# A fused encoder layer on one core: one weight unit's low parts go to VectorE, a low part and its products go ahead of a scaling, and the gates' product goes two units later

## The chip, the cores and the metric

One core of one Trainium2 chip runs the whole kernel. The metric is the device time of one execution in microseconds, as the median of three runs: 691.59 us before the change (691.51 to 693.78). All times below count from the start of the span of the profiled execution, in us, unless they are durations.

The engines are TensorE (PE in the profile), VectorE (DVE), ScalarE (ACT), GpSimd (POOL) and SyncE (SP), which here only issues transfers.

## The reference, cut to what matters

The layer normalises x, projects it by one wide matrix, runs two token mixers and merges them. The change touches the normalisation, the first group of projected columns (sq, the attention's queries) and the gates mi and mf.

```python
h = rmsnorm(x, norm_w)                       # x: 512 tokens of 1024 channels, float32
proj = jnp.einsum('bsd,de->bse', h, w_in) + b_in
(mq, mk, mv, mi, mf, mo, mz, sq, sk, sv, sz, gates) = jnp.split(proj, split_at, axis=-1)
...
log_i = mi.astype(jnp.float32).transpose(0, 2, 1)
log_f = jax.nn.log_sigmoid(mf.astype(jnp.float32)).transpose(0, 2, 1)
...
qs = rmsnorm(to_heads(sq, SB_HEADS), sb_q_norm_w)
ks_ = rmsnorm(to_heads(sk, SB_HEADS), sb_k_norm_w)
os_ = stick_breaking_attention(qs, ks_, to_heads(sv, SB_HEADS))
```

## The kernel before

**Tiles and products.** The 512 tokens are four blocks (tb = 0 to 3) of 128; the 1024 channels are eight slices (k = 0 to 7) of 128. Every float32 operand is split into a high part in a rounded format and a low part, the rest; a product of two operands is three matmuls of 512 columns (high by high and the two mixed ones). The normalised and turned x lies in `hh` (high) and `hl` (low). Weights are fetched in units of 512 KB into `stg` (three buffers); ACT copies the high part (`wh`), DVE subtracts the low part (`wl`), lines 97 and 98.

**The head.** The first group (units 0 to 3, queries of attention heads 0 to 3) is special: each unit holds two slices k, `first_split` (L1141) makes their high parts `fh` on ACT and their low parts `fl` on DVE for units 0 and 2, on POOL for units 1 and 3 (L1147). Unit 3 is fetched into a buffer with the tag P5, so its tile reads `P`. Per block of x, `x_scale` (L277) has ACT make the sum of squares, POOL the reciprocal root (`rstd`, L274 and L275, result in `xs`) and DVE scale x in place (L290). `x_turn` (L292) has PE transpose the block in eight pieces (L300, into two PSUM tiles `aps`), DVE make `hh` (L302, four slices at once) and `hl` (L306, one slice at a time).

**The order.** All is written out by hand: each engine runs its instructions in the order in which the code issues them, and waits there for what it needs. The code issues the work ahead of the loop (L1149 to L1177), then loops over the units c = 0, 1, 2, ...: evacuation of unit c-1's sums, deferred functions due at c, fetches and splits up to unit c+2 (`ahead`), the first half of unit c's products (`mm(0)`), waiting pieces, the attention heads' steps, the second half (`mm(1)`). In the head, unit c's products are block tb = c over all eight k (`first_mm`, L1181): k = 0 to 3 in `mm(0)`, 4 to 7 in `mm(1)`. `x_turn(1)` stands between the halves of c = 0, and behind it `x_scale(2)` and `x_scale(3)`; `x_turn(2)` and `x_turn(3)` stand in c = 1. The sums of the first group get a bias row `brow`, fetched from DRAM, on DVE (L347, `qraw`).

**The gates.** `gates_prep` (due at c = 3) makes the high and low part of the gates' weights (`wg`) on DVE. `gates` (due at c = `GATES_START`, 4) runs 16 matmuls (L573, L574), one copy on ACT (L576), one sum on DVE (L578), and two stores to DRAM issued by SP (`i_d` and `f_d`, L580 and L581). Those are read again at c = 35 (`gates_scan`).

**Behind it on SP.** The queries are turned for the attention in two parts: DVE transposes 32 by 32 blocks (`ty`, L388), one unit later SP issues sixteen small transfers (`tz`, L398), and still later DVE multiplies `tz` by a weight `qkw` (L402). The first part's `tz` are issued at c = 6, the second's at c = 8. Units 4 to 7 are the keys `kraw`; DVE scales them by their norm `rk` (L369, eight instructions for two blocks, twice). At c = 10 the first head starts: PE transposes the four blocks of `kraw` (L438) between the halves of unit 10.

Of the kernel before, what the change touches and what calls it, by code (L numbers as in the profile page):

```python
# [8 lines left out]
F32 = mybir.dt.float32  # L9
FR = mybir.dt.float32r  # L10
BF = mybir.dt.bfloat16
AF = mybir.ActivationFunctionType
OP = mybir.AluOpType
# [3 lines left out]
KT = 8  # L17
# [8 lines left out]

SB_START = [10, 13, 16, 20, 26, 28, 32, 34]
M_START = [52, 56, 70, 76]
GATES_PREP, GATES_START, GATES_SCAN = 3, 4, 35
TURNED = {("q", 0, 0), ("q", 0, 1), ("q", 1, 0), ("q", 1, 1), ("k", 0, 1), ("k", 1, 1)}  # L30
REST = {11, 16, 20, 23, 24, 32, 44, 64}
AHEAD, LOADS = 2, 4
# [3 lines left out]
def tile_hybrid_layer(  # L36
# [16 lines left out]
    nc = tc.nc  # L53
# [21 lines left out]
    def blk(tag, dt=F32, shape=(512,), name=None, p=128):  # L75

        where = mp if tag in MISC else sp
        return where.tile([p] + list(shape), dt, name=name or tag, tag=tag, bufs=BUFS[tag])

    def two(tag, dt=F32, name=None):  # L80

        t = blk(tag, dt, (2, 512), name=name)
        return t[:, 0, :], t[:, 1, :]

    def dense_ps():
        return psd.tile([128, 512], F32, name="dps", tag="dps")

    def att_ps():
        return psa.tile([128, 512], F32, name="aps", tag="aps")
# [40 lines left out]
    units = []  # L130
# [59 lines left out]
    def h_sta(k, tb):  # L190
        ts = slice(tb * 128, (tb + 1) * 128)
        return hh[:, k, ts], hl[:, k, ts]
# [8 lines left out]
    x_t = []  # L201
# [16 lines left out]
    ident = cst.tile([128, 128], F32, name="ident")  # L218
# [8 lines left out]
    nw_t = cst.tile([128, 8], F32, name="nw_t")  # L227
# [42 lines left out]
    hh = hp.tile([128, KT, T], FR, name="hh", tag="hh")  # L270
    hl = hp.tile([128, KT, T], FR, name="hl", tag="hl")

    def rstd(dst, ssq, n, eps):
        nc.gpsimd.tensor_scalar(dst, ssq, 1.0 / n, eps, op0=OP.mult, op1=OP.add)  # L274
        nc.gpsimd.tensor_tensor(dst, dst, mhalf[:, 0:dst.shape[1]], op=OP.pow)  # L275

    def x_scale(tb):  # L277
        xs = tiny.tile([128, 4], F32, name="xs", bufs=2)
        ssq, r = xs[:, 0:2], xs[:, 2:3]
        xn = x_t[tb]  # L280
        junk = blk("om", BF, (D,), name="junk")
        if tb == 0:
            for i in range(2):
                c = slice(i * D // 2, (i + 1) * D // 2)
                nc.scalar.activation(junk[:, c], xn[:, c], AF.Square, accum_out=ssq[:, i:i + 1])
            nc.gpsimd.tensor_tensor(ssq[:, 0:1], ssq[:, 0:1], ssq[:, 1:2], op=OP.add)
        else:
            nc.scalar.activation(junk, xn, AF.Square, accum_out=ssq[:, 0:1])
        rstd(r, ssq[:, 0:1], D, EPS)
        nc.vector.tensor_scalar(xn, xn, r, None, op0=OP.mult)  # L290

    def x_turn(tb):  # L292
        ts = slice(tb * 128, (tb + 1) * 128)
        xn = x_t[tb]
        for g in range(2):
            ks = slice(4 * g, 4 * g + 4)
            tp = att_ps()
            for j in range(4):
                kt = g * 4 + j
                nc.tensor.transpose(tp[:, j * 128:(j + 1) * 128], xn[:, kt * 128:(kt + 1) * 128], ident)  # L300
            dh = hh[:, ks, ts]
            nc.vector.tensor_tensor(dh, tp.rearrange("p (k t) -> p k t", k=4),  # L302
                                    nw_t[:, ks].unsqueeze(2).to_broadcast([128, 4, 128]), op=OP.mult)
            for j in range(4):
                k = 4 * g + j
                nc.vector.scalar_tensor_tensor(hl[:, k, ts], tp[:, j * 128:(j + 1) * 128], nw_t[:, k:k + 1],  # L306
                                               hh[:, k, ts].bitcast(F32), op0=OP.mult, op1=OP.subtract)

    def bias_row(c0):
        b = blk("brow")  # L310
# [242 lines left out]
    def gates_fill():  # L553
        wg = blk("P5", FR, (KT, 128), name="wg")
        nc.gpsimd.memset(wg.bitcast(F32), 0.0)
        wg_t.append(wg)
# [513 lines left out]
    u = []  # L1070
# [67 lines left out]

    f_w = []

    def first_split(i, low=None):  # L1141
        u = units[i]
        his = two("qk", FR, name="fh")
        for j in range(2):
            hi, lo = his[j], blk("y", FR, name="fl")
            nc.scalar.activation(hi, u.st[:, j, :], AF.Copy)
            (low or nc.vector).tensor_tensor(lo, u.st[:, j, :], hi.bitcast(F32), op=OP.subtract)  # L1147
            f_w.append((hi, lo))

    units[0].load()  # L1150
    units[1].load()
# [12 lines left out]
    def warm(n):  # L1164
        for _ in range(n):
            nc.tensor.matmul(wp, idle[:, 0:128], idle, start=True, stop=True)

    warm(9)
    norm_vec()
    x_scale(0)  # L1170
    warm(2)
    first_split(0)
    x_turn(0)
    first_split(1, nc.gpsimd)
    x_scale(1)
    first_split(2)
    first_split(3, nc.gpsimd)  # L1177

    f_ps = []

    def first_mm(tb):  # L1181
        def mm(half):
            if half == 0:
                f_ps.append(dense_ps())
            for k in range(4 * half, 4 * half + 4):
                sh, sl = h_sta(k, tb)
                wh, wl = f_w[k]
                nc.tensor.matmul(f_ps[tb], sh, wh, start=k == 0, stop=False)
                nc.tensor.matmul(f_ps[tb], sl, wh, start=False, stop=False)
                nc.tensor.matmul(f_ps[tb], sh, wl, start=False, stop=k == KT - 1)  # L1190
        return mm
# [36 lines left out]
    def ahead(c):  # L1228
        while count["ready"] < min(N, c + AHEAD + 1):
            fetch(count["ready"] + 1)  # L1230
            units[count["ready"]].split()
            count["ready"] += 1
        fetch(c + LOADS + 1)

    for c in range(N):
        now[0] = c
        if 0 < c < TB:
            ahead(c)
        if c and units[c - 1].slow:
            units[c - 1].slow()  # L1240
            ahead(c)
        due = later.pop(c, [])
        if c > n_proj - 9:
            ahead(c)
        if c:
            units[c - 1].evac()
        for fn in due:
            fn()
        ahead(c)
        units[c].mm(0)  # L1250
        if c < 2:
            x_turn(c + 1)
        if c == 0:
            x_scale(2)
            x_scale(3)
            gates_fill()
        for g in list(act):
            if c in REST:
                continue
            if next(g, "end") == "end":  # L1260
                act.remove(g)
        for e in list(pend):
            if c >= e[0] and e[2]():
                pend.remove(e)
                g = e[3]()
                next(g)
                act.append(g)
        units[c].mm(1)
        if c == 1:
            x_turn(3)  # L1270
# [31 lines left out]
```

## Time and profile before

| | us |
|---|---|
| median of three runs | 691.59 |
| lowest and highest run | 691.51, 693.78 |
| the profiled execution's own time | 692.46 |
| its span | 690.7 |
| PE busy | 682.2 |
| DVE busy | 467.5 |
| ACT busy | 337.1 |
| POOL busy | 115.3 |

The span goes from the first to the last instruction. Busy time of PE counts matmuls that overlap once; a matmul of 512 columns is shown with some 0.39 us, but the next one starts 0.23 us after it. A row of the timeline gives the start, the duration, the engine, the line, the operation and its operands, and in brackets the idle time of the engine ahead of it with what ended it, if that is known; `x8` are eight such instructions in a row.

### The profile page before, as it was taken

How to read it: one execution, taken by the hardware profiler on the slowest of the kernel's cores; microseconds unless marked ns; L12 is line 12 of the kernel's file. 1: busy time of each engine (PE TensorE's matmuls, PEld its weight loads, DVE VectorE, ACT ScalarE, POOL GpSimd, SP SyncE). 2: the span in 40 equal slices, each digit the busy share in tenths (PEclk: the TensorE clock that was granted, in tenths of full speed). 3: DMA queues.
4: the chain of work that ended last, by engine and by line, in shares of the span. 5: the costliest groups of instructions: out<-in, count | busy, mean ns of one | idle time of the engine just before them, and what ended most of it. 6: DMA issues, size and time to landing. Idle time of an engine off the chain costs nothing.

```text
span 690.7 us, 9388 instructions
## 1 busy us (share of the span) xinstructions
PE 682.2 (99%) x3162; PEld 568.9 (82%) x3162; DVE 467.5 (68%) x817; ACT 337.1 (49%) x631; POOL 115.3 (17%) x268
## 2 busy tenths in 40 slices
PE   7999999999999999999999999999999999999997
PEld 4878888888888888888888888888888888888876
DVE  6745687777997886679834748994352364445997
ACT  6235364576554663244466434447554343344451
POOL 5222022365440310000011110000112000111020
PEclk9999999999999999999999999999999999999999
DMA  7423534535553533553332333434323455489333
GB/s 249 138 92 107 155 108 127 148 71 151 158 149 106 135 106 90 112 121 92 106 108 61 91 105 104 117 92 125 88 62 91 113 179 196 135 194 222 121 82 102
DMA packets 122289, 84.74 MB, mean 123 GB/s; under 512 B 19018, under 2 KB 105956, under 8 KB 122240
## 3 DMA queue, kind: packets, MB, share of 16 engines
q1 hardware_dynamic: 119600, 77.97, 40.2%
q0 software_dynamic: 2496, 6.03, 4.5%
q8 instruction: 25, 0.41, 0.2%
q14 instruction: 24, 0.20, 0.1%
q10 hardware_dynamic: 144, 0.13, 0.1%
HBM read 66.22 MB, written 2.15 MB: 99 GB/s over the span
## 4 chain that ended last, share of the span: by engine, by line
PE 94%; DMA 2%; DVE 2%; POOL 1%; SPq 0%; ACT 0%; issue 0%; DVEq 0%; ACTq 0%
PE dps L92 27%; PE dps L93 27%; PE dps L94 27%; PE aps L93 3%; PE aps L94 3%; PE aps L92 3%; DMA P<-in_w_in_dram 1%; DMA brow<-in_b_in_dram 1%; PE aps L794 1%; PE aps L796 1%; PE aps L795 1%; DVE hl L306 1%; POOL fl L1147 0%; DVE hh L302 0%; DVE wl L98 0%; PE aps L573 0%
## 5 line engine op out<-in xcount | busy, mean ns | idle before, releaser
L98 DVE TENSOR_TENSOR wl<-stg,wh 128x1024 fp32r<-128x1024 f32 x92 | 112.6, 1224 | 107.6 <-ACT wh L97 107.4
L92 PE MATMUL dps<-hh,wh 128*128 128x512 f32 x448 | 175.0, 391 | 0.0
L94 PE MATMUL dps<-hh,wl 128*128 128x512 f32 x448 | 174.4, 389 | 0.0
L93 PE MATMUL dps<-hl,wh 128*128 128x512 f32 x448 | 174.4, 389 | 0.0
L97 ACT ACTIVATE wh<-stg 128x1024 fp32r<-128x1024 f32 x92 | 96.8, 1052 | 65.3 <-PE dps L94 45.1
L94 PEld LDWEIGHTS dps<-hh,wl 128*128 128x128 f32 x448 | 84.1, 188 | 17.7
L93 PEld LDWEIGHTS dps<-hl,wh 128*128 128x128 f32 x448 | 84.2, 188 | 16.8
L92 PEld LDWEIGHTS dps<-hh,wh 128*128 128x128 f32 x448 | 84.1, 188 | 16.8
L92 PE MATMUL dps<-wh,hh 128*128 128x512 f32 x224 | 87.7, 392 | 0.0
L94 PE MATMUL dps<-wh,hl 128*128 128x512 f32 x224 | 87.3, 390 | 0.0
L93 PE MATMUL dps<-wl,hh 128*128 128x512 f32 x224 | 87.2, 389 | 0.0
L94 PEld LDWEIGHTS dps<-wh,hl 128*128 128x128 f32 x224 | 42.0, 188 | 9.0
L92 PEld LDWEIGHTS dps<-wh,hh 128*128 128x128 f32 x224 | 42.1, 188 | 8.3
L93 PEld LDWEIGHTS dps<-wl,hh 128*128 128x128 f32 x224 | 42.1, 188 | 8.2
L687 DVE SCALAR_TENSOR_TENSOR acc<-tmp,vec,acc 128x511 f32<-128x511 f32 (+2 forms) x48 | 36.0, 750 | 1.7
L690 ACT ACTIVATE tmp<-acc 128x512 f32<-128x512 f32 x16 | 10.1, 634 | 50.8 <-DVE acc L687 50.8
L463 POOL TENSOR_SCALAR_AFFINE_SELECT om<-om 128x128 f32<-128x128 f32 x32 | 15.3, 479 | 96.2 <-ACT om L461 96.1
L469 DVE TENSOR_TENSOR_SCAN om<-om 128x512 f32<-128x512 f32 (+3 forms) x32 | 26.7, 834 | 5.5 <-POOL om L463 5.5
L747 POOL TENSOR_SCALAR_AFFINE_SELECT w_all<-om 128x128 f32<-128x128 f32 x16 | 5.7, 386 | 143.6 <-DMA om<-rb_d 129.4
L461 ACT ACTIVATE om<-aps,rq 128x512 f32<-128x512 f32 (+3 forms) x32 | 16.8, 524 | 21.0 <-PE aps L94 21.0
L92 PE MATMUL dps<-yh,wh 128*128 128x512 f32 x64 | 24.9, 389 | 0.0
L93 PE MATMUL dps<-yl,wh 128*128 128x512 f32 x64 | 24.9, 389 | 0.0
(249 smaller groups left out, 1222.2 us busy)
## 6 DMA issues: line engine op xcount, KB each, us to landing
stg<-in_w_in_dram SPq DMA_DIRECT2D x87, 512.0 KB, 3.9
az<-ay SPq DMA_DIRECT2D x128, 40.0 KB, 3.2
stg<-in_w_proj_s_dram SPq DMA_DIRECT2D x8, 512.0 KB, 4.3
B<-in_w_out_dram SPq DMA_DIRECT2D x8, 512.0 KB, 5.8
stg<-in_w_proj_m_dram SPq DMA_DIRECT2D x8, 512.0 KB, 5.5
wl<-stg POOLq DMA_DIRECT2D x8, 512.0 KB, 5.8
tz<-ty SPq DMA_DIRECT2D x72, 32.0 KB, 1.9
brow<-in_b_in_dram SPq DMA_DIRECT2D x8, 256.0 KB, 4.4
```

The lines of the kernel that those rows point to most:

```text
L92: nc.tensor.matmul(ps, ah, bh, start=first, stop=False)
L93: nc.tensor.matmul(ps, ah, bl, start=False, stop=False)
L94: nc.tensor.matmul(ps, al, bh, start=False, stop=last)
L97: nc.scalar.activation(hi, src, AF.Copy)
L98: nc.vector.tensor_tensor(lo, src, hi.bitcast(F32), op=OP.subtract)
L306: nc.vector.scalar_tensor_tensor(hl[:, k, ts], tp[:, j * 128:(j + 1) * 128], nw_t[:, k:k + 1], hh[:, k, ts].bitcast(F32), op0=OP.mult, op1 ...
L461: nc.scalar.activation(om[:, 0:n], zp, AF.Sigmoid, scale=rn[:, h:h + 1])
L463: nc.gpsimd.affine_select(out=om[:, ts], in_=om[:, ts], compare_op=OP.is_gt, fill=1.0, base=0, channel_multiplier=1, pattern=[[-1, 128]])
L469: nc.vector.tensor_tensor_scan(back, back, back, 1.0, op0=OP.mult, op1=OP.bypass)
L687: nc.vector.scalar_tensor_tensor(acc[:, j:], t[:, 0:T - j], cw(3 - j, ch), acc[:, j:], op0=OP.mult, op1=OP.add)
L690: nc.scalar.activation(t, acc, AF.Sigmoid)
L794: nc.tensor.matmul(nm[:, 0:258], ph, vh, start=j == 0, stop=False)
```

## The change

Three things. The low parts of unit 3 (k = 6 and 7) are made by DVE in place of POOL. One low part (k = 4) stands on DVE ahead of the scaling of block 1, and the products of k = 4 stand on PE ahead of the transposes of block 1; the scaling of block 2 stands on DVE between the two halves of block 1's `hh` and `hl`, in place of behind both, and the transposes of block 2 follow behind `mm(0)` of c = 1 as before. The gates' product with all that it issues is due at c = 6 in place of 4. To this end `x_scale` and `x_turn` are cut into pieces that do the same work. In the diff, lines that only rename are left out.

```diff
-GATES_PREP, GATES_START, GATES_SCAN = 3, 4, 35
+GATES_PREP, GATES_START, GATES_SCAN = 3, 6, 35
...
     def x_scale(tb):
+        x_norm(tb)
+        x_mul(tb)
+
+    def x_norm(tb):
...
         rstd(r, ssq[:, 0:1], D, EPS)
-        nc.vector.tensor_scalar(xn, xn, r, None, op0=OP.mult)
+        x_r.append(r)
+
+    def x_mul(tb):
+        nc.vector.tensor_scalar(x_t[tb], x_t[tb], x_r[tb], None, op0=OP.mult)
...
+    def x_tp(tb, g):
+        tp = x_ps[tb, g] = att_ps()
+        for j in range(4):
+            kt = g * 4 + j
+            nc.tensor.transpose(tp[:, j * 128:(j + 1) * 128], x_t[tb][:, kt * 128:(kt + 1) * 128], ident)
+
+    def x_hh(tb, g):
...
+    def x_hl(tb, *ks):
...
     def x_turn(tb):
...
+            x_tp(tb, g)
+            x_hh(tb, g)
+            x_hl(tb, *range(4 * g, 4 * g + 4))
...
+    def first_hi(i):
         his = two("qk", FR, name="fh")
         for j in range(2):
...
+            nc.scalar.activation(his[j], units[i].st[:, j, :], AF.Copy)
+            f_w.append((his[j], blk("y", FR, name="fl")))
+
+    def first_lo(k, engine=nc.vector):
+        hi, lo = f_w[k]
+        engine.tensor_tensor(lo, units[k // 2].st[:, k % 2, :], hi.bitcast(F32), op=OP.subtract)
...
-    first_split(0)
+    first_hi(0)
+    first_lo(0)
+    first_lo(1)
     x_turn(0)
-    first_split(1, nc.gpsimd)
-    x_scale(1)
-    first_split(2)
-    first_split(3, nc.gpsimd)
+    first_hi(1)
+    first_lo(2, nc.gpsimd)
+    first_lo(3, nc.gpsimd)
+    x_norm(1)
+    first_hi(2)
+    first_lo(4)
+    x_mul(1)
+    first_lo(5)
+    first_hi(3)
+    first_lo(6)
+    first_lo(7)
...
-            for k in range(4 * half, 4 * half + 4):
+            n = 4 if tb else 5
+            for k in range(n) if half == 0 else range(n, KT):
...
         units[c].mm(0)
-        if c < 2:
-            x_turn(c + 1)
         if c == 0:
-            x_scale(2)
+            x_tp(1, 0)
+            x_tp(1, 1)
+            x_hh(1, 0)
+            x_hl(1, 0, 1, 2, 3)
+            x_norm(2)
+            x_mul(2)
+            x_hh(1, 1)
+            x_hl(1, 4, 5, 6, 7)
             x_scale(3)
             gates_fill()
+        if c == 1:
+            x_turn(2)
```

What the change does to the order is shown at two places. Line numbers of the changed kernel are higher: the scaling L290 is L297 there, fl L1147 is L1166, hh L302 is L309, hl L306 is L317, qraw L347 is L364, the stores of the gates L580 and L581 are L597 and L598, tz L398 is L415, the bias row L311 is L328.

DVE in the head, from hl of block 0 to the first bias sum. Before:

```order
L306 SCALAR_TENSOR_TENSOR hl<-aps,nw_t,hh 128x128 x4
L290 TENSOR_SCALAR x<-x,xs 128x1024
L1147 TENSOR_TENSOR fl<-stg,fh 128x512 x2
L302 TENSOR_TENSOR hh<-aps,nw_t 128x4x128
L306 SCALAR_TENSOR_TENSOR hl<-aps,nw_t,hh 128x128 x4
L302 TENSOR_TENSOR hh<-aps,nw_t 128x4x128
L306 SCALAR_TENSOR_TENSOR hl<-aps,nw_t,hh 128x128 x4
L290 TENSOR_SCALAR x<-x,xs 128x1024 x2
L347 TENSOR_TENSOR qraw<-dps,brow 128x512
```

After:

```order
L317 SCALAR_TENSOR_TENSOR hl<-aps,nw_t,hh 128x128 x4
L1166 TENSOR_TENSOR fl<-stg,fh 128x512
L297 TENSOR_SCALAR x<-x,xs 128x1024
L1166 TENSOR_TENSOR fl<-stg,fh 128x512
L1166 TENSOR_TENSOR fl<-P_121,fh 128x512 x2
L309 TENSOR_TENSOR hh<-aps,nw_t 128x4x128
L317 SCALAR_TENSOR_TENSOR hl<-aps,nw_t,hh 128x128 x4
L297 TENSOR_SCALAR x<-x,xs 128x1024
L309 TENSOR_TENSOR hh<-aps,nw_t 128x4x128
L317 SCALAR_TENSOR_TENSOR hl<-aps,nw_t,hh 128x128 x4
L297 TENSOR_SCALAR x<-x,xs 128x1024
L364 TENSOR_TENSOR qraw<-dps,brow 128x512
```

One low part moved ahead of the scaling of block 1, two (of `P`, unit 3) came over from POOL, and the scaling of block 2 moved between the two hh of block 1.

SP from the last of the small loads of the head to the weight loads of units 12 and 13 (`stg` are weight loads, `brow` bias rows, `i_d` and `f_d` the gates' stores, `tz` the turned queries). Before:

```order
L117 DMA stg<-in_w_in_dram 128x2x512 x4
L580 DMA i_d<-g_488 4x512
L581 DMA f_d<-g_488 4x512
L117 DMA stg<-in_w_in_dram 128x2x512 x2
L311 DMA brow<-in_b_in_dram 128x512
L398 DMA tz<-ty 32x2x128 x16
L117 DMA stg<-in_w_in_dram 128x2x512 x2
L398 DMA tz<-ty 32x2x128 x16
L117 DMA stg<-in_w_in_dram 128x8x128 x2
```

After:

```order
L117 DMA stg<-in_w_in_dram 128x2x512 x6
L328 DMA brow<-in_b_in_dram 128x512
L597 DMA i_d<-g_559 4x512
L598 DMA f_d<-g_559 4x512
L415 DMA tz<-ty 32x2x128 x16
L117 DMA stg<-in_w_in_dram 128x2x512 x2
L415 DMA tz<-ty 32x2x128 x16
L117 DMA stg<-in_w_in_dram 128x8x128 x2
```

The gates' stores moved behind two weight loads and a bias row, and stand straight ahead of the first sixteen tz.

## Rows read from the trace of the kernel before

**Rows 1.** The page: span, and PE's busy time (us, share of the span, instructions).

```profile
span 690.7 us, 9388 instructions
PE 682.2 (99%) x3162; PEld 568.9 (82%) x3162; DVE 467.5 (68%) x817; ACT 337.1 (49%) x631; POOL 115.3 (17%) x268
```

**Rows 2.** The waits of PE over the whole span: who waited for what, us in total, times, longest us.

```profile
PE dps L1166 <- DVE idle L1161: 1.5, 1, 1.5
PE aps L300 <- DVE x L290: 1.4, 2, 1.2
PE dps L1188 <- DVE hh L302: 0.8, 1, 0.8
PE dps L1190 <- DVE fl L1147: 0.7, 1, 0.7
PE aps L573 <- DVE wg L563: 0.4, 1, 0.4
```

**Rows 3.** The timeline of PE in the head: the last product of k = 3, the transposes of block 1, the first product of k = 4, the last product of block 0 and the first of block 1, and the first of block 2.

```profile
11.74 0.50 PE L1190 MATMUL dps<-fl,hh 128*128 128x512 f32 x1
13.45 1.09 PE L300 MATMUL aps<-ident,x 128*128 128x128 f32 x8 [1.20 <-DVE x L290]
14.30 0.47 PE L1188 MATMUL dps<-fh,hh 128*128 128x512 f32 x1
...
18.32 0.39 PE L1190 MATMUL dps<-fl,hh 128*128 128x512 f32 x1
18.55 0.39 PE L1188 MATMUL dps<-fh,hh 128*128 128x512 f32 x1
...
25.69 0.48 PE L1188 MATMUL dps<-fh,hh 128*128 128x512 f32 x1
```

**Rows 4.** The timeline of DVE in the head: unit 0's low parts, the scaling of block 1, unit 2's low parts, hl of block 1, the first bias sum and hh of block 2.

```profile
6.83 1.29 DVE L1147 TENSOR_TENSOR fl<-stg,fh 128x512 fp32r<-128x512 f32 x2
...
12.64 0.75 DVE L290 TENSOR_SCALAR x<-x,xs 128x1024 f32<-128x1024 f32 x1 [1.00 <-POOL xs L275]
13.31 3.46 DVE L1147 TENSOR_TENSOR fl<-stg,fh 128x512 fp32r<-128x512 f32 x2
...
17.41 1.12 DVE L306 SCALAR_TENSOR_TENSOR hl<-aps,nw_t,hh 128x128 fp32r<-128x128 f32 x4
...
22.55 0.69 DVE L347 TENSOR_TENSOR qraw<-dps,brow 128x512 f32<-128x512 f32 x1 [0.94 <-DMA brow<-in_b_in_dram]
23.16 0.68 DVE L302 TENSOR_TENSOR hh<-aps,nw_t 128x512 fp32r<-128x512 f32 x1
```

**Rows 5.** The same stretch of ACT (high parts of unit 2) and POOL (the second step of rstd for block 1, low parts of unit 3).

```profile
10.92 1.15 ACT L1146 ACTIVATE fh<-stg 128x512 fp32r<-128x512 f32 x2
12.05 0.56 POOL L275 TENSOR_TENSOR xs<-xs,mhalf 128x1 f32<-128x1 f32 x1
12.90 3.32 POOL L1147 TENSOR_TENSOR fl<-P,fh 128x512 fp32r<-128x512 f32 x2 [0.30 <-ACT fh L1146]
```

**Rows 6.** The timeline of PE around the gates' product: the last product of block 3, the first of the gates, the first of unit 4 and of unit 5.

```profile
36.97 0.39 PE L1190 MATMUL dps<-fl,hh 128*128 128x512 f32 x1
37.77 0.47 PE L573 MATMUL aps<-hh,wg 128*128 128x512 f32 x1 [0.41 <-DVE wg L563]
...
41.50 0.39 PE L92 MATMUL dps<-wh,hh 128*128 128x512 f32 x1
...
46.94 0.39 PE L92 MATMUL dps<-wh,hh 128*128 128x512 f32 x1
```

**Rows 7.** SP: its longest wait on an engine up to 110 us, then its timeline (the duration runs from the first issue to the end of the last).

```profile
SPq L580 <- DVE g L578: 11.2, 1, 11.2
...
43.10 0.28 SPq L580 DMA_DIRECT2D i_d<-g  x1
...
45.86 11.03 SPq L398 DMA_DIRECT2D tz<-ty  x16
56.99 1.04 SPq L117 DMA_DIRECT2D stg<-in_w_in_dram  x2
58.14 10.59 SPq L398 DMA_DIRECT2D tz<-ty  x16
...
68.14 0.58 SPq L398 DMA_DIRECT2D tz<-ty  x1
...
80.31 10.18 SPq L398 DMA_DIRECT2D tz<-ty  x16
```

**Rows 8.** The page's DMA issues: KB each and the median us from issue to landing, over the whole span.

```profile
stg<-in_w_in_dram SPq DMA_DIRECT2D x87, 512.0 KB, 3.9
...
tz<-ty SPq DMA_DIRECT2D x72, 32.0 KB, 1.9
```

**Rows 9.** The timeline around the first head: DVE's multiplication of the second tz and scaling of the second half of kraw, PE's transposes of kraw in the middle of unit 10 and the first product of unit 10's second half.

```profile
71.13 0.75 DVE L402 TENSOR_SCALAR tz<-tz,qkw 128x1024 f32<-128x1024 f32 x1
71.80 1.65 DVE L369 TENSOR_SCALAR kraw<-kraw,rk 128x128 f32<-128x128 f32 x8
...
76.86 0.60 PE L438 MATMUL aps<-ident,kraw 128*128 128x128 f32 x4
77.22 0.48 PE L92 MATMUL dps<-wh,hh 128*128 128x512 f32 x1
```

**Rows 10.** The timeline of PE at the start of the span: products on an idle tile.

```profile
1.50 4.21 PE L1166 MATMUL dps<-idle 128*128 128x512 f32 x9 [1.50 <-DVE idle L1161]
```

More of the change, by code (lines that the diff above doesn't have):

```diff
@@ L289, in x_scale @@
         rstd(r, ssq[:, 0:1], D, EPS)
-        nc.vector.tensor_scalar(xn, xn, r, None, op0=OP.mult)
+        x_r.append(r)
+    def x_mul(tb):
+        nc.vector.tensor_scalar(x_t[tb], x_t[tb], x_r[tb], None, op0=OP.mult)
+    x_r, x_ps = [], {}
+    def x_tp(tb, g):
[4 more added lines that the diff above has]
+    def x_hh(tb, g):
+        ks = slice(4 * g, 4 * g + 4)
+        nc.vector.tensor_tensor(hh[:, ks, tb * 128:(tb + 1) * 128],
+                                x_ps[tb, g].rearrange("p (k t) -> p k t", k=4),
+                                nw_t[:, ks].unsqueeze(2).to_broadcast([128, 4, 128]), op=OP.mult)
+    def x_hl(tb, *ks):
+        ts = slice(tb * 128, (tb + 1) * 128)
+        for k in ks:
+            tp = x_ps[tb, k // 4][:, k % 4 * 128:k % 4 * 128 + 128]
+            nc.vector.scalar_tensor_tensor(hl[:, k, ts], tp, nw_t[:, k:k + 1],
+                                           hh[:, k, ts].bitcast(F32), op0=OP.mult, op1=OP.subtract)
     def x_turn(tb):
-        ts = slice(tb * 128, (tb + 1) * 128)
-        xn = x_t[tb]
         for g in range(2):
[L296 to L307, printed above, removed]
+            x_tp(tb, g)
+            x_hh(tb, g)
+            x_hl(tb, *range(4 * g, 4 * g + 4))
     def bias_row(c0):
@@ L1139, in tile_hybrid_layer @@
     f_w = []
-    def first_split(i, low=None):
-        u = units[i]
+    def first_hi(i):
         his = two("qk", FR, name="fh")
         for j in range(2):
[L1145 to L1148, printed above, removed]
+            nc.scalar.activation(his[j], units[i].st[:, j, :], AF.Copy)
[3 more added lines that the diff above has]
+        engine.tensor_tensor(lo, units[k // 2].st[:, k % 2, :], hi.bitcast(F32), op=OP.subtract)
     units[0].load()
```

## The prediction

> **What bounds the kernel now.** I read the page first. TensorE (PE) is busy 682.2 of 690.7 us [rows 1], so only time in which PE stands still, or work added to it, can move the end. The list of PE's waits then says where it stands still: 1.5 us before the first product, 1.4 on a scaled block of x, 0.8 on hh, 0.7 on a low part fl, 0.4 on wg, and nothing else in the whole span [rows 2]. The last of these is the one on wg, ahead of the gates' product; from there on PE starts a product every 0.23 us to the end. So the change can win only in the first 38 us, and what it wins arrives at the end unless it makes a new wait later. I therefore read the head engine by engine [rows 3 to 6], and then, since the gates' product is moved and SP, the queue that issues the loads, sends its result, SP's own timeline [rows 7].
>
> **The head: what is in the way.** In the first block PE stops after k = 3 at 11.74 and resumes at 13.45 with the transposes of block 1, which wait for DVE's scaling; it then runs twelve products from 14.30 and starts block 1 at 18.55 [rows 3]. Twelve products at 0.23 would take 2.8 us, not 4.25: DVE's two low parts of the third unit take 3.46 us from 13.31, where the same pair took 1.29 at 6.83 [rows 4]. In the slow pair's time POOL makes the fourth unit's two low parts, 12.90 to 16.22 [rows 5].
>
> **Low part k = 4 ahead of the scaling.** The scaling starts at 12.64, after 1.00 us in which DVE stood waiting for POOL's rstd [rows 4], which ends at 12.61 [rows 5]. fh for k = 4 is there about 11.5 (two copies from 10.92 take 1.15) [rows 5], so one subtraction of some 0.65 us runs from 11.64 to 12.3 in that idle stretch and moves nothing: the scaling stays at 12.64, the transposes at 13.45. PE's three products of k = 4, 12.1 to 12.8, lie in PE's gap of 1.7 us. Cost nothing, as long as rstd comes no sooner.
>
> **Fourth unit's low parts on DVE.** POOL loses 3.32 us, DVE gains two subtractions. After the scaling (ends 13.39) DVE makes three at about 0.65 each: 14.0, 14.65, 15.3. After the transposes PE has nine products left from 14.30, nine steps of 0.23 and a tenth of a us that the first takes longer behind transposes, so it starts block 1 at about 16.45. It uses k = 5, 6, 7's low parts at about 14.8, 15.5 and 16.2, each after it is ready. Against 18.55 that is **2.1 us sooner**. If POOL's absence gave DVE nothing (low parts still at 1.73 each) the three would end at 18.6 and the 2.1 would be lost; with 0.65 measured alone in the same operation, I take 2.1.
>
> **Third block scaled sooner, hh and hl of block 1 later.** DVE goes 15.3, hh (0.68) 16.0, four hl (1.13) 17.1, x_mul(2) 17.8, hh 18.5, hl 19.7, x_mul(3) 20.4. PE needs hh at 16.45, the first hl a step later, transposes of block 2 at 19.2, hl for k = 4 at 20.2: no wait. But then a fixed date comes: qraw waits for the bias row from DRAM, which lands just before 22.55, and hh of block 2 stands behind it in DVE's order, 23.16 to 23.85 [rows 4]. No instruction ahead of that transfer on SP is moved. PE, 2.1 us sooner, would start block 2 at 23.6 in place of 25.69 [rows 3] and waits until 23.9. **0.3 us is given back**; 1.8 stays.
>
> **Gates' product two units later.** Before, PE ends block 3 at 37.20 (36.97 and 0.23) and starts the gates' product at 37.77, held by wg [rows 6]. With it moved behind unit 5, unit 4 follows block 3 directly and this 0.57 us is gone too; its 16 products (3.73 us, 37.77 to 41.50) are only moved. Unit 4 starts at 35.4, unit 5 (5.44 each, 41.50 to 46.94 [rows 6]) at 40.8, the gates at 46.3, unit 6 at 49.9. Unit 6 started at 52.38 (41.50 and two units), so PE is now **2.4 us ahead**.
>
> **What is moved past on SP.** The product takes its readers along: ACT's copy, DVE's sum, and SP's i_d and f_d, which wait for that sum. SP stood 11.2 us on it before [rows 7]. In the new order three loads pass ahead of i_d, but the sixteen transfers tz stand behind it. Before, i_d went out at 43.10, 1.83 us after the start of the last gates' product (41.50 less 0.23), and tz began at 45.86 [rows 7]. Now that product starts at 49.7, i_d goes at 51.5, and behind it and f_d, each 0.28 and a little [rows 7], tz begins at **52.2, 6.35 us later**, while PE is 2.4 sooner. Behind tz nothing on SP can catch up: from 45.86 on it issues without standing still, sixteen tz in 11.03, two loads, sixteen more in 10.59 from 58.14, some 0.64 to 0.69 a piece, and a third sixteen later take 10.18 [rows 7]. So the last tz of the second sixteen moves from 68.14 to 74.5, and lands 1.9 us later [rows 8], at 76.4 in place of 70.0.
>
> **Who waits for that.** DVE multiplies the second tz by qkw at 71.13, without having waited, and only behind that, in its order, scales the second half of kraw, done at 73.45 [rows 9]. PE transposes kraw in the middle of unit 10, at 76.86, and goes on with unit 10's second half at 77.22 [rows 9]: 3.4 us of cover. Now DVE waits for the landing, starts at 76.4 and has kraw scaled 2.32 us later (71.13 to 73.45), at 78.7. PE is there at 74.4, can do two of its four transposes, and resumes the products at about 78.9. So PE stands still for some 4.1 us, and the 2.4 us are more than gone: 78.9 against 77.22 is **1.7 us later than before**. The cover of 3.4 us cannot hold a shift of 6.35 and 2.4; only the 1.1 us between landing and use help.
>
> The load of unit 10, at 56.99 behind the first tz [rows 7], moves to 63.3 and lands by some 67.5 (3.9 median [rows 8]); its two split passes end about 70, PE needs them at 71.7 (twelve products ahead of the transposes at 76.86 [rows 9], so 74.1, less 2.4). Just in time, and a short delay there would be swallowed by the stall behind it. Later loads move by the same 6 us once; the stall gives PE's distance back to them.
>
> **The sum.** Profiled execution: 692.46 us (span 690.7 and 1.8 around it), less 2.1, plus 0.3, less 0.6, plus 4.1: 694.2. It lies 0.87 above the median of 691.59, so the median should come to **693.3 us**. Bounds of this case: at the third sixteen's pace (10.18 for each in place of 11.03 and 10.59) the chain is 1.3 shorter, net plus 0.4; as much again on the other side by half, 0.7, is net plus 2.4. On the median that is 692.0 to 694.0.
>
> **Rivals.**
> *The gain stays.* Were PE not held in unit 10, the time would be 691.59 - 2.4 = 689.2. For it: all steps of the head rest on durations measured alone. Against it: the chain through SP would have to be 4.1 us shorter than worked out, and three sixteens at nearly the same pace speak against that. 10%.
> *Slower side: PE's clock falls in the stall.* PE's products went at 0.43 us each until about 5.6 us (nine in 4.21), which is 512 columns at 1.2 GHz, and at 0.23, the 2.4 GHz level, afterwards [rows 10]. The pause of 1.7 us in the head was followed by products at 0.23 again [rows 3], so a pause of that length left the clock alone; no row shows one of 4. If it falls, and takes as long to rise as at the start (4.1 us from 1.50), PE loses 4.1 x (1 - 0.23/0.43) = 1.9 us more: 695.2. It decides from the pause's length, and two lone transposes fall into it. 12%. The Trainium skill, "TensorE: Matmul & The Clock Gate", section "Why this matters for your kernels", warns that an idle gap between matmul bursts drops the clock back to its lower level; by that rule the time would be this rival's 695.2, by the head's pause of 1.7 us it is 693.3, and no run here shows a gap so long.
> *The change does not free the head.* If the low parts stay slow on DVE, gates, i_d and tz come up to 1.8 us later, one for one, and so does PE's resumption in unit 10, which hangs on that chain alone: up to 695.1. 5%.
>
> **How the numbers follow.** Forecast 693.3 with 70%, own range 692.0 to 694.0; gain stays 10%; clock 12%; head not freed 5%; other 3%. The range 690.9 to 695.6 holds the forecast, the two slow rivals and part of the smaller stalls. About 0.5% (3.5 us) is what a measurement of this kernel can tell from no change: faster than 688.1 would take more than the head has to give (4%), slower than 695.05 takes the clock or a head not freed with it (11%), the rest, 85%, lies between.
>
> **What would show it.** Right: fl at about 0.65 each on DVE, block 1 at 16.4, PE waiting once for hh near 23.9, no wait on wg; SP's i_d at 51.5 and tz from 52; DVE's tz multiplication held by a transfer until about 76.4; PE's transposes of kraw waiting some 4 us, products at 0.23 after them. Wrong: no wait of PE after 24 us (the gain stays), products at 0.43 after 79 us (the clock), tz issued sooner than 52, or a wait at unit 10's start on its split instead.

## The result and the profile after

After the change the time is 694.12 us (median of 19 runs, 692.97 to 696.38), against 691.91 for the kernel before in the runs beside them: ratio 1.0034, 95% interval 1.0026 to 1.0043. It is slower by 2.2 us, where 1.7 had been worked out. The wide bracket of 690.9 to 695.6 holds it; the forecast's own range of 692.0 to 694.0 misses it by 0.1.

The profiled execution took 695.65 us. The page of the changed kernel (span; PE's busy time), then the list of PE's waits (who waited for what: us in total, times, longest):

```profile
span 693.9 us, 9386 instructions
PE 684.1 (99%) x3162; PEld 570.4 (82%) x3162; DVE 467.0 (67%) x819; ACT 337.4 (49%) x631; POOL 113.2 (16%) x266
```

```profile
PE aps L455 <- DVE kraw L386: 2.6, 2, 2.1
PE dps L1184 <- DVE idle L1179: 1.5, 1, 1.5
PE aps L305 <- DVE x L297: 0.9, 1, 0.9
PE dps L1216 <- DVE hh L309: 0.8, 1, 0.8
PE dps L94 <- DMA wl<-stg: 0.6, 1, 0.6
```

Against [rows 2] the waits on fl and wg are gone, and a new one, on kraw, stands at the top. PE's busy time also rose by 1.9 us [rows 1] with the same 3162 matmuls: some of them ran longer. The chain behind the new wait is the one forecast. SP stands 8.4 us at the first store, waiting for the gates' sum. Its wait there, then SP's timeline (start, duration from the first issue to the end of the last), and DVE's two instructions at the chain's end:

```profile
SPq L597 <- DVE g L595: 8.4, 1, 8.4
```

```profile
51.82 0.28 SPq L597 DMA_DIRECT2D i_d<-g  x1
...
52.48 10.33 SPq L415 DMA_DIRECT2D tz<-ty  x16
...
64.06 10.58 SPq L415 DMA_DIRECT2D tz<-ty  x16
...
74.06 0.59 SPq L415 DMA_DIRECT2D tz<-ty  x1
```

```profile
76.20 0.75 DVE L419 TENSOR_SCALAR tz<-tz,qkw 128x1024 f32<-128x1024 f32 x1 [2.65 <-DMA tz<-ty]
76.87 1.65 DVE L386 TENSOR_SCALAR kraw<-kraw,rk 128x128 f32<-128x128 f32 x8
```

The first tz goes out at 52.48 in place of 45.86 [rows 7], and DVE's multiplication, which waited for nothing at 71.13 [rows 9], now waits 2.65 us for the transfer. The timeline of PE there: the transposes of kraw, the first products behind them, and the products a microsecond later.

```profile
74.71 0.38 PE L455 MATMUL aps<-ident,kraw 128*128 128x128 f32 x2
77.20 0.33 PE L455 MATMUL aps<-ident,kraw 128*128 128x128 f32 x1 [2.12 <-DVE kraw L386]
77.99 0.33 PE L455 MATMUL aps<-ident,kraw 128*128 128x128 f32 x1 [0.46 <-DVE kraw L386]
78.07 0.48 PE L92 MATMUL dps<-wh,hh 128*128 128x512 f32 x1
...
79.42 0.63 PE L94 MATMUL dps<-wh,hl 128*128 128x512 f32 x1
79.84 0.63 PE L92 MATMUL dps<-wh,hh 128*128 128x512 f32 x1
...
82.40 0.49 PE L92 MATMUL dps<-wh,hh 128*128 128x512 f32 x1
82.73 0.39 PE L93 MATMUL dps<-wl,hh 128*128 128x512 f32 x1
```

PE resumes at 78.07, 0.85 later than the 77.22 of [rows 9]. Then, from 79.42 to 82.40, seven products start 0.43 us apart and not 0.23; the step into this stretch and the one out of it take 0.33 each. That is 7 x 0.20 + 2 x 0.10 = 1.6 us more, and it is where the longer matmuls lie. The same two stretches by windows (busy us of PE, PEld, DVE, ACT and POOL with counts, then the granted clock, the DMA share and GB/s):

```profile
74.70:78.07 3.37, 0.80 (x5) 0.36 (x4) 1.87 (x8) 0.00 (x0) 0.00 (x0) 1.00 0.70 171
78.07:82.50 4.43, 4.43 (x14) 3.48 (x15) 3.18 (x8) 2.18 (x3) 0.00 (x0) 0.63 1.05 301
```

The granted clock is 1.00 in the pause itself and 0.63 on average over the products behind it: a stretch at the lower level of 1.2 GHz. The first product of unit 12 starts at 87.97, before at 85.51: 0.85 and 1.6. The last wait in the list, near 646 us, adds some 0.8 more in this execution. It appears in the profiles of late_pool_low and late_k4_back below too and not in the others, so it is left out of the account; why it comes is open.

The head after the change (PE, then DVE, then POOL):

```profile
14.06 1.09 PE L305 MATMUL aps<-ident,x 128*128 128x128 f32 x8 [0.88 <-DVE x L297]
...
17.07 0.39 PE L1216 MATMUL dps<-fh,hh 128*128 128x512 f32 x1
```

```profile
11.83 0.69 DVE L1166 TENSOR_TENSOR fl<-stg,fh 128x512 fp32r<-128x512 f32 x1
13.25 0.75 DVE L297 TENSOR_SCALAR x<-x,xs 128x1024 f32<-128x1024 f32 x1 [0.73 <-POOL xs L275]
```

```profile
12.02 0.56 POOL L274 TENSOR_SCALAR xs<-xs 128x1 f32<-128x1 f32 x1
12.66 0.56 POOL L275 TENSOR_TENSOR xs<-xs,mhalf 128x1 f32<-128x1 f32 x1
```

Block 1 starts at 17.07, 1.5 us sooner than the 18.55 of [rows 3] and 0.6 later than forecast, because the scaling starts at 13.25 and not at 12.64 [rows 4].

### The profile page after: what moved, and what is told of

Read it like the earlier page. It is cut to its first block, busy times and chain, and to the rows that moved or that the text cites. A ratio compares the mean times of both kernels' runs of the same rounds, so it can differ in the third digit from the quotient of the medians.

```text
span 693.9 us, 9386 instructions
## 1 busy us (share of the span) xinstructions
PE 684.1 (99%) x3162; PEld 570.4 (82%) x3162; DVE 467.0 (67%) x819; ACT 337.4 (49%) x631; POOL 113.2 (16%) x266
## 4 chain that ended last, share of the span: by engine, by line
PE 92%; DMA 3%; SPq 2%; issue 1%; POOL 1%; DVE 0%; ACT 0%; DVEq 0%; ACTq 0%
PE dps L92 26%; PE dps L94 26%; PE dps L93 26%; PE aps L93 3%; PE aps L94 3%; PE aps L92 3%; SPq L415 2%; DMA stg<-in_w_in_dram 2%; DMA wl<-stg 1%; PE dps L1216 1%; PE dps L1218 1%; PE dps L1217 1%; PE aps L811 1%; PE aps L813 1%; PE aps L812 1%
## 5 line engine op out<-in xcount | busy, mean ns | idle before, releaser
L94 PE MATMUL dps<-yh,wl 128*128 128x512 f32 x64 | 25.0, 391 | 0.6 <-DMA wl<-stg 0.6
```

Of the source, the lines that this page charges most:

```text
L94: nc.tensor.matmul(ps, al, bh, start=False, stop=last)
```

## The experiments

All theories share the head and differ on the loss. **Theory S**: SP issues in order, so the stores i_d and f_d, which wait for the gates' sum, hold everything queued behind them. **Theory C**: on top of that, PE's clock falls behind the pause that S makes. **Rival**: the gates' product is worse placed late, whatever SP does. The table has every run; before is the median of the runs of before on the same chip.

| kernel | median us | lowest, highest | before | ratio, 95% interval |
|---|---|---|---|---|
| the change | 694.12 | 692.97, 696.38 | 691.91 | 1.0034, 1.0026 to 1.0043 |
| stores_late | 689.63 | 689.35, 690.0 | 691.53 | 0.9971, 0.9959 to 0.9982 |
| gates_only | 696.6 | 694.66, 697.17 | 691.53 | 1.0064, 1.0051 to 1.0078 |
| gates_back | 691.18 | 690.77, 693.35 | 691.53 | 0.9999, 0.9991 to 1.0008 |
| warm_gap | 692.66 | 692.14, 693.34 | 691.53 | 1.0013, 1.0004 to 1.0021 |
| gates_at_7 | 690.3 | 689.58, 690.84 | 692.2 | 0.9970, 0.9959 to 0.9981 |
| late_pool_low | 691.31 | 689.92, 692.91 | 692.2 | 0.9984, 0.9976 to 0.9993 |
| late_k4_back | 690.47 | 689.66, 690.79 | 692.2 | 0.9970, 0.9958 to 0.9982 |
| late_gates_4 | 692.18 | 691.59, 694.0 | 692.2 | 1.0006, 0.9996 to 1.0016 |
| late_bias_early | 690.14 | 689.13, 691.15 | 691.8 | 0.9970, 0.9959 to 0.9980 |
| stores_late_again | 689.74 | 689.06, 692.91 | 691.8 | 0.9971, 0.9961 to 0.9980 |

### The stores deferred: stores_late

The change whole, but the two stores are issued three units later than the sum that they store.

```diff
-        nc.sync.dma_start(i_d, g2[0:4, :])
-        nc.sync.dma_start(f_d, g2[32:36, :])
+        def store():
+            nc.sync.dma_start(i_d, g2[0:4, :])
+            nc.sync.dma_start(f_d, g2[32:36, :])
+
+        defer(3, store)
```

> The changed kernel, but the gates' two stores are issued three units later, behind both sixteens of tz. Theory S (SP stands on the gates' sum ahead of tz, and that alone holds PE in unit 10): tz starts near 44 instead of 52.5, PE does not wait for kraw, the clock stays at its upper level, and the 2.2 us that PE was ahead before unit 10 reach the end: about 689.7, 2.2 below before. Rival H (the moved gates' product or the denser head itself costs time later on, whatever stands on SP): still 693 to 695.

PE's whole list of waits, then SP:

```profile
PE dps L1187 <- DVE idle L1182: 1.5, 1, 1.5
PE dps L1219 <- DVE hh L309: 1.2, 1, 1.2
PE aps L305 <- DVE x L297: 0.4, 2, 0.2
```

```profile
42.57 10.94 SPq L415 DMA_DIRECT2D tz<-ty  x16
...
54.77 10.20 SPq L415 DMA_DIRECT2D tz<-ty  x16
...
65.92 0.47 SPq L598 DMA_DIRECT2D i_d<-g  x1
```

Nothing on PE, DVE, ACT or POOL was moved, and the wait on kraw is gone: the first tz goes out at 42.57 and not 52.48, even 3.3 us ahead of before's 45.86. 689.63 is 2 us under before, so the version beats both kernels. Run again on another chip (stores_late_again) it gave the same ratio. Theory S is shown.

> The change with the stores deferred once more, on the same chip as the run with the early bias row: 0.997 of before, 689.6 us where before takes 691.5, no wait of PE on kraw.

One of that second set, the profiled one, took 692.91; it tells of the clock, in the last section.

### The product one unit later still: gates_at_7

```diff
-GATES_PREP, GATES_START, GATES_SCAN = 3, 6, 35
+GATES_PREP, GATES_START, GATES_SCAN = 3, 7, 35
```

> The change whole, with the gates' product one unit later still (due at c = 7), so that the two stores stand behind the first sixteen tz on SP and not ahead of them. If the loss comes from the stores' place on SP alone, a later product costs nothing: the first tz from about 42.6, i_d at some 57, the second sixteen issued by about 69 and landed by 71, no wait of PE on kraw, 689.7 us (689.2 to 690.4), as with the stores deferred. Rival: the product's place late among the units is what hurts (its copy and sum on ACT and DVE beside the keys' work, PE's products interrupted), then it is no better than at c = 6: 694 or more, with a wait on kraw or the clock below 1.

```profile
43.24 11.25 SPq L415 DMA_DIRECT2D tz<-ty  x16
...
56.60 0.29 SPq L597 DMA_DIRECT2D i_d<-g  x1
...
57.97 10.64 SPq L415 DMA_DIRECT2D tz<-ty  x16
```

A product and a sum that come later still cost nothing, once the stores stand behind the first tz in SP's order: 0.9970, the same as with the stores deferred, and no wait on kraw. The rival falls. c = 6 was bad for its place on SP alone.

### The gates' move alone: gates_only

The kernel before with that one number changed.

```diff
-GATES_PREP, GATES_START, GATES_SCAN = 3, 4, 35
+GATES_PREP, GATES_START, GATES_SCAN = 3, 6, 35
```

> The kernel before with one number changed: gates at unit 6 instead of 4, nothing else of the change. Theory S: the head stays as before, PE saves the 0.6 us wait on wg, i_d goes out about 1.5 us later than in the changed kernel (its head is 1.5 us slower), so PE resumes in unit 10 near 79.5 instead of 77.2, some 2.3 us behind before, plus up to 1.7 us of lower clock: 694 to 696. Rival H: without the edits of the head nothing is lost, 691.3 to 692.

```profile
53.49 10.35 SPq L398 DMA_DIRECT2D tz<-ty  x16
```

```profile
78.36 0.33 PE L438 MATMUL aps<-ident,kraw 128*128 128x128 f32 x1 [2.27 <-DVE kraw L369]
79.15 0.33 PE L438 MATMUL aps<-ident,kraw 128*128 128x128 f32 x1 [0.46 <-DVE kraw L369]
79.23 0.49 PE L92 MATMUL dps<-wh,hh 128*128 128x512 f32 x1
```

Without the faster head everything in the chain is 1.0 to 1.2 us later than in the change (tz at 53.49, PE back at 79.23), and the time is the worst of all, 696.6, above the 694 to 696 expected. This is what the prediction had for a head that is not freed: the resumption hangs on SP's chain alone. The profiled execution (694.66) kept its clock behind the same stall: granted 1.00 over its products from 79.23 to 84.00. The two runs with a mean granted clock of 0.999 took 694.66 and 694.77, the four with 0.997 or 0.998 took 696.44 to 697.17.

### The pause filled: warm_gap

The change, with nine products into a spare tile between the second and the third transpose of kraw; their sums are not used.

```diff
+                        if tb == 2 and name == "k" and self.s == 0 and h == 0:
+                            wk = att_ps()
+                            for _ in range(9):
+                                nc.tensor.matmul(wk, hh[:, 0, 0:128], hh[:, 0, :], start=True, stop=True)
```

> The changed kernel, with nine extra products of 512 columns into an unused PSUM tile between the second and third transpose of kraw in unit 10 (their result is never read), 2.1 us of work inside PE's wait of 2.4 us. Theory C (the rest of the loss, and the spread of the runs, is the clock at 1.2 GHz behind that wait): no product at 0.43 us after the wait, PE resumes at the same 78.1, time 692.9 to 693.4 in all runs, about 1 below the changed kernel. Rival (the clock has nothing to do with this wait): 693 to 696 spread as in the changed kernel, or later by what the nine products take.

```profile
73.95 2.31 PE L458 MATMUL aps<-hh 128*128 128x512 f32 x9
...
77.28 0.48 PE L92 MATMUL dps<-wh,hh 128*128 128x512 f32 x1
```

```profile
77.28:81.70 4.42, 4.42 (x21) 3.65 (x22) 3.27 (x8) 3.24 (x4) 0.00 (x0) 1.00 1.01 299
```

The granted clock behind the pause is 1.00, and 21 instructions take the time of the change's 14. All eleven runs have a mean clock of 0.999 or 1.000. Against the change the ratio falls from 1.0034 to 1.0013, some 1.5 us, for work that computes nothing. On the same chip gates_only, with a like pause unfilled, has a mean clock of 0.998 or less in four of six runs. Theory C is shown. The profile alone would not carry the 1.5, since its chain on SP and DVE ran 0.8 sooner (multiplication at 75.41); the runs' ratio and clock do. What remains over before, 0.9 us by the ratio, is of the size of the stall's net 0.85. This profile does not show it: PE resumes at 77.28 (78.1 expected), 0.06 behind before.

### The gates' product at its old place: gates_back, late_gates_4

The change, and the change with the stores deferred, each with `GATES_START` 4.

> The changed kernel with the gates back at unit 4: only the edits of the head. Theory S: tz goes out as before and PE does not wait for kraw, but PE now waits longer for wg, whose date (37.6) hangs on DVE and the bias row, so the head's 1.5 us are lost there: 691.9, the same as before, with a wait of about 2 us on wg. Rival (the head's gain is kept once the gates are back): 690.4.

> The change with the stores deferred and the gates' product at its old place (c = 4). If the gates' move is what lets the head's gain through (ahead of the product PE waits for wg, which DVE and the bias row set and the head's gain doesn't move), PE waits 1.0 to 1.5 us on wg and the time is that of the change with the gates back, about 691.2 (690.6 to 691.5). Rival: the deferred stores give something of their own, by tz going out sooner, then it is 689.6 to 690.2 here too.

PE's longest wait in gates_back, then in late_gates_4, then late_gates_4 by windows around it:

```profile
PE aps L590 <- DVE wg L580: 1.4, 1, 1.4
```

```profile
PE aps L590 <- DVE wg L580: 2.0, 1, 2.0
```

```profile
34.58:36.95 2.37, 0.39 (x2) 0.03 (x1) 2.30 (x10) 0.96 (x5) 0.71 (x1) 1.00 0.27 29
36.95:42.29 5.34, 5.34 (x17) 4.23 (x17) 0.46 (x1) 2.26 (x12) 2.90 (x6) 0.68 0.23 85
```

With the product in its old place the head's gain does not reach the end: PE comes sooner and waits longer for wg (0.4 before [rows 2]). The date of wg hangs on the bias row. On DVE wg stands behind a low part wl, which waits 2.8 us for ACT's high part, and in all twelve profiles that wl starts 12.24 to 12.27 us behind the first bias sum qraw (qraw and wl at 22.55 and 34.80 before, 21.20 and 33.45 in gates_back, 21.74 and 33.98 in late_gates_4). In these three profiles qraw waited for the bias row, which the head's edits do not bring sooner: it came at 22.54 in the change. Of the two kernels here, the one where it came 0.54 later has the wait of 2.0 and not 1.4. Both times are level with before. The waits lie on either side of what was expected (about 2 for gates_back, 1.0 to 1.5 for late_gates_4), and late_gates_4's 692.18 lies above its 690.6 to 691.5, on a chip where before takes 692.2. In late_gates_4's profile that wait was followed by the lower clock as well (0.68), 5 of its 11 runs have a mean clock of 0.998 or less and took 693.15 to 694.0, the other six 691.59 to 692.18; with the gates back it was 3 of 12. So the gates' move is needed, for more than the 0.57 us of wg that the prediction gave it: it lets the head through. The rival of late_gates_4, that the deferred stores give something by themselves, falls.

### The head in parts: late_pool_low, late_k4_back, late_bias_early

All three start from stores_late (0.9971).

```diff
-    first_lo(6)
-    first_lo(7)
+    first_lo(6, nc.gpsimd)
+    first_lo(7, nc.gpsimd)
```

> The change with the stores deferred (689.63, 0.9971 of before, in its own run), and the fourth unit's low parts back on POOL. If POOL's subtraction slows DVE's beside it, fl of k = 5 takes about 1.7 us on DVE from 13.3 in place of 0.65, is done at 15.05 where PE wants it at 14.75, and hh of block 1 comes later too: block 1 starts 0.3 to 0.6 later, 690.0 to 690.3 us. Rival: the fourth unit's move is the whole of the head's gain, then block 1 starts at 18.5 and the time is 691.3 to 691.8. Second rival: PE's order hides it all, 689.6.

```profile
13.11 1.75 DVE L297 TENSOR_SCALAR x<-x,xs 128x1024 f32<-128x1024 f32 x1 [0.72 <-POOL xs L275]
14.78 1.75 DVE L1169 TENSOR_TENSOR fl<-stg,fh 128x512 fp32r<-128x512 f32 x1
```

```profile
13.04 2.95 POOL L1169 TENSOR_TENSOR fl<-P,fh 128x512 fp32r<-128x512 f32 x2
```

0.9984, about 0.9 us worse than stores_late: by the middle of the runs the fourth unit's move is worth some 0.9 us, between the first guess and the rival, but the intervals overlap from 0.9976 to 0.9982, so its size is not settled. In the profiled execution, the slowest of the twelve, almost the whole head is lost (block 1 at 18.28), for not only fl but the scaling too takes 1.75 beside POOL's subtraction, in place of 0.75; that depends on when POOL starts. The scaling also starts 0.6 later than in stores_late, for a reason given below (the head).

```diff
-    first_lo(4)
     x_mul(1)
+    first_lo(4)
...
-            n = 4 if tb else 5
+            n = 4
```

> The change with the stores deferred, and the low part of k = 4 and its products back behind the scaling and the transposes of block 1. PE then has twelve products behind the transposes in place of nine: block 1 starts three steps of 0.23 us later, 0.7, and 690.1 to 690.4 us come out, if no wait later in the head takes that 0.7 in both. Rival: hh of block 2, behind the bias row, holds PE in both, so nothing is lost: 689.6 to 689.8.

0.9970: no loss that can be measured. In the profiles block 1 starts at 16.70 here and at 16.36 in stores_late, with the scaling at 12.21 and 12.54: by that the part for k = 4 is worth 0.3 to 0.7 us. It also has a price of its own (below); that this price eats the gain over the runs is not shown. The rival's time came without its cause: PE did not wait for hh of block 2 in either profile.

```diff
+    early = {}
+
     def bias_row(c0):
+        if c0 in early:
+            return early.pop(c0)
...
     load_x(3)
+    early[C_SQ] = bias_row(C_SQ)
```

> The change with the stores deferred, and the first bias row issued on SP ahead of the gates' weights and the small rows (from 6.6 us in place of 17). If the landing of the bias row is the fixed date that holds hh of block 2 (PE waited 1.2 us for it with the stores deferred), that wait goes, qraw runs on DVE as soon as the scaling of block 3 is done, about 20.6, block 2 starts some 1.0 to 1.2 us sooner, and the time is 688.4 to 688.8 where the deferred stores alone give 689.6. Rival: PE runs into the next thing at once (weights of unit 4, or hl of block 2 on DVE), and it is the same time as with the stores deferred alone.

0.9970, no gain; and the expectation was wrong in its reading. The wait on hh of 1.2 us in stores_late's list stands at 9.25 in the timeline, ahead of the first product of block 0, and not at block 2:

```profile
9.25 0.47 PE L1219 MATMUL dps<-fh,hh 128*128 128x512 f32 x1 [1.15 <-DVE hh L309]
```

A line in the list of waits says which code waited, not when. The bias row was not in PE's way here: in stores_late qraw still waited 0.77 for it, at 21.32, and PE did not. It holds PE where the gates' product follows block 3 at once, as in gates_back and late_gates_4 above.

## Why the prediction was right, and where it was off

**Sign, place and cause were right**, step for step: unit 6 at 50.22 (49.9 worked out, where the terms add up to 50.0; 2.16 ahead of before in place of 2.4), i_d at 51.82 (51.5), tz from 52.48 (52.2), the multiplication at 76.20 (76.4), two of four transposes done before the stall, no product waiting on wg. The stores on SP are shown as the cause, by stores_late and gates_at_7.

**The stall was mis-sized: "some 4.1 us", net 1.7 later.** It measured 3.0, net 0.85. Two terms make the difference. The sixteen tz took 10.33 and 10.58 for 11.03 and 10.59; they started 0.3 later, and from the last issue to the multiplication 2.1 us passed in place of 1.9, so the landing came 0.2 sooner. And the prediction let PE wait for all eight scalings of kraw (done at 76.87 + 1.65 = 78.52), while PE's last transpose started at 77.99: it needs the first head's columns of each block alone, the fifth of the eight. That is 0.6, and it could have been read from the code: the eight go block by block and head by head.

**The clock was given 12% and came in most runs.** Products at 0.43 after 79 us were named as a sign of being wrong, and the profile has seven of them. Of the change's 19 runs 13 have a mean granted clock of 0.998 or less, median 694.63; the six with 0.999 or 1.000 have 693.27, beside the forecast of 693.3. That nearness is partly luck: before's median is 0.3 higher here than the 691.59 that the forecast started from, the net stall was half as long and the head gave less; of the 1.4 us that these six lie above before, the profiled stall explains 0.85, and the rest is open. The likeliest case was the rival with the clock, sized 1.9 us there and 1.6 in the profile. The reason against it was a row of another pause, the 1.7 us in the head that left the clock alone; but from 74.71 to 78.07 PE had four lone transposes and nothing else, twice as long. The pause's length does not decide alone, as the rival had it: gates_only's profile kept its clock behind 3.5 us of the same kind. The section of the Trainium skill that the prediction named ("TensorE: Matmul & The Clock Gate", "Why this matters for your kernels") warns of an idle gap between bursts. The trace of the change agrees, with a granted clock of 0.63 over the 4.43 us behind the gap; that of gates_only, at 1.00 behind its gap, does not.

**The head: "2.1 us sooner", "cost nothing, the scaling stays at 12.64".** The sum holds where nothing disturbs it: block 1 starts at 16.36 in stores_late (16.45 worked out). In the profile of the change it starts at 17.07. The low part put ahead of the scaling runs on DVE at 11.83 while POOL makes rstd at 12.02, and the first of rstd's two small instructions (L274) takes 0.56 in place of 0.19; the second (L275) takes 0.56 with or without it [rows 5]. Started 0.25 later than before as well, rstd puts the scaling 0.6 back. In stores_late POOL comes first:

```profile
11.49 0.19 POOL L274 TENSOR_SCALAR xs<-xs 128x1 f32<-128x1 f32 x1
```

In late_bias_early and late_pool_low the two meet again (0.64, 0.56); in the other profiles with this low part L274 is done before it starts (0.19). So this step is not free: it depends on which comes first. The scaling of block 2 was mis-sized too, 1.17 in the change for 0.75, beside POOL's filling of a tile of 128x1024; PE did not wait for it.

**"0.3 us is given back" at hh of block 2 did not happen.** Block 2 starts at 24.20 without a wait, 7.13 behind block 1's 17.07, as far apart as before. In the change the bias row came when it was put (qraw at 22.54, hh done at 23.83), but PE, 0.6 late from the scaling, came behind it. Nor is the bias row a fixed date: DVE had it at 21.32 in stores_late.

## What to carry to other kernels

When a computation is moved later, look at what its result issues: a store waiting for its value in an in-order queue holds every transfer behind it, and it can be issued later at no cost if nobody reads it soon. When a pause of PE is priced, price the products behind it at the lower clock too. When an engine arrives sooner, ask what sets the date of the next thing that it needs: here the landing of a bias row, some 15 us and a chain of instructions ahead of wg. And find the time of each wait before building on it; a list by line does not give it.

## What the runs showed of the hardware

- The clock fell behind pauses of different kinds: the kraw stall of the change (waits of 2.12 and 0.46 us with single transposes), the wait of 2.0 us on wg in late_gates_4, and, in the profiled run of stores_late_again (692.91), a wait of 2.38 at a late start of the head, with a granted clock of 0.51 from 10.43 to 16.60. It is not certain: gates_only's profile had 2.27 and 0.46 and stayed at 1.00, and so did gates_back's behind a wait of 1.4. Nine products in the pause kept it at 1.00 in warm_gap. A run's mean clock does not say where it fell: before, with none of these stalls in its profile, has 0.998 or less in none of 24 runs on one chip and in 3 of 24 and 4 of 19 on another. Timeline of the late head in stores_late_again, PE:

```profile
10.43 0.77 PE L1219 MATMUL dps<-fh,hh 128*128 128x512 f32 x1 [2.38 <-DVE hh L309]
11.00 0.63 PE L1220 MATMUL dps<-fh,hl 128*128 128x512 f32 x1
...
16.12 0.58 PE L1220 MATMUL dps<-fh,hl 128*128 128x512 f32 x1
16.54 0.40 PE L1221 MATMUL dps<-fl,hh 128*128 128x512 f32 x1
```

- DVE and POOL slow each other, on large and on tiny operations: DVE's subtraction of 128x512 takes 0.69 without POOL's and 1.75 beside it, its scaling 0.75 and 1.75, and POOL's L274 on 128x1 takes 0.19 alone and 0.56 to 0.64 where it meets DVE's subtraction at block 1. The Trainium skill, "GPSIMD Engine Reference", section "1. Specifications", lists the SBUF interfaces as shared with VectorE, with contention where a DVE instruction has two SBUF inputs or runs in a 2-port perf mode. The subtraction has two, and the trace agrees. The scaling has one tensor input, and does 1024 columns in 0.75 where the subtraction does 512 in 0.69; that would fit the second case, but no run here shows the mode.
